# Lower halves of a mixer's weights: a subtraction on VectorE against a scaled copy on ScalarE and an adding DMA

## The chip, the cores and the metric

The program runs on one core of a Trainium2 chip. The metric is the device time of one execution in microseconds, the median of a few runs. TensorE (PE in the rows) multiplies matrices, its weight loads (PEld) run beside the multiplications, VectorE is DVE, ScalarE is ACT, GpSimd is POOL, SyncE is SP.

## The reference

A trunk of two layers over one sequence of 512 tokens with 1024 channels, all in float32. Each layer is

```python
x = x + 0.5 * swiglu_ffn(rmsnorm(x, ffn1_norm[l]), ffn1_w_up[l], ffn1_w_down[l])
x = x + mixer(rmsnorm(x, mix_norm[l]), ...)
x = x + 0.5 * swiglu_ffn(rmsnorm(x, ffn2_norm[l]), ffn2_w_up[l], ffn2_w_down[l])
x = rmsnorm(x, final_norm[l])
```

The mixer multiplies its input with one wide matrix `w_in`, whose columns are q, k and v (three dilation groups of eight heads, 64 wide), the two halves of a gated linear unit (GLU), and two gates, A for the attention branch and one for the convolution branch. Attention is a dilated sliding window. The convolution branch is GLU, a depthwise convolution over 31 tokens, a LayerNorm, a swish and a projection. At the end:

```python
g_attn, g_conv = jnp.split(jax.nn.sigmoid(gates), 2, axis=-1)
return (g_attn * y_attn + g_conv * y_conv) @ w_out
```

## The kernel before, in words

**Three products for one.** TensorE multiplies in a rounded float32 (`F32R`). To keep precision, each operand is split into an upper half, the value rounded, and a lower half, what the rounding left. `mm3` (lines 156 to 159) issues three matmuls for every product: upper times upper, upper weight times lower activation, lower weight times upper activation, all into one accumulator.

**A stage.** Weights come from HBM in pieces of 128 partitions by 1024 numbers (512 KB), that is four row blocks of 256 columns or eight of 128. `stage` (line 140) handles one piece: SyncE's queue issues the load into `raw` (line 151, two buffers), ScalarE copies it rounded into `hi` (line 152, four buffers), VectorE subtracts, `lo = raw - hi` (line 153, four buffers). A stage feeds 24 matmuls of 512 columns. All of it stands under `tc.high_priority(offset=150)`.

**Who calls it.** `proj_cols` (line 218) walks over the row blocks and calls `stage` and `mm3`; the feed-forward layers, the GLU's input, the gates and the three output projections use it or the same loop. `tokens_chunk`, for q, k and v, calls `stage` directly, with two sources side by side for q and k.

**The order of the mixer in the program.** (1) The GLU's input, four column pairs, gate half first (`ps_gg`, `ps_ga`, lines 279 to 292): 16 stages. (2) For each dilation group q, k, v and attention: small matmuls, a masked minimum on VectorE (line 437), the exponential on ScalarE (line 443), transposes, and stores and loads through HBM on GpSimd's queue (`vd`, `V`, `od`, `sd`). (3) The convolution's gate (`ps_gc`), then gate A (`ps_gA`), 8 stages each, with a sigmoid (lines 490 and 503). (4) The depthwise convolution on VectorE, 31 steps for each of 8 blocks (line 516), and the LayerNorm. (5) The attention's parts come back from HBM (`oin`, line 572) and are joined. (6) The convolution's projection (`ps_cp`, 8 stages), attention's (`ps_ap`, 4) and the output's (`ps_o`, 8).

**The order on the chip.** The order within each engine's queue is not the program's: a planner simulates a timeline with a cost for each instruction and writes each engine's queue by priority (place in the program, less the offset above) and by when inputs are ready in that simulation. On the chip each queue then runs strictly in that order. So the convolution's steps stand scattered through VectorE's queue from the GLU on, and the gates' matmuls lie among attention's. Buffers are let go when their last reader is done.

Of the kernel before, what the change touches and what calls it, by code (L numbers as in the profile page):

```python
# [11 lines left out]
F32 = mybir.dt.float32  # L12
F32R = mybir.dt.float32r
AF = mybir.ActivationFunctionType
ALU = mybir.AluOpType
# [4 lines left out]
P = 128  # L20
D = 1024
S = 512
KD = D // P
# [6 lines left out]
AW = NG * NH * HD  # L30
# [14 lines left out]
def trunk(ctx: ExitStack, tc: tile.TileContext, A: dict, out: bass.AP):  # L45
    nc = tc.nc
# [7 lines left out]
    def ps_mm(name):  # L54
        return psp.tile([P, S], F32, tag="mm", name=name, bufs=3)

    def ps_st(name):
        return psp.tile([P, S], F32, tag="st", name=name, bufs=1)

    def ps_at(name):  # L60
        return psp.tile([P, S], F32, tag="at", name=name, bufs=4)
# [63 lines left out]
    def pc(nm, l, k):  # L125
        i = VECS.index(nm) * 16 + l * 8 + k
        return pcol[:, i:i + 1]
# [8 lines left out]
    def uniq(s):  # L136
        cnt[0] += 1
        return f"{s}_{cnt[0]}"

    def stage(*srcs):  # L140

        a, n1 = srcs[0].shape[1], srcs[0].shape[2]
        n = n1 * len(srcs)
        raw = wp.tile([P, 1024], F32, tag="raw", name=uniq("raw"), bufs=2)
        hi = wp.tile([P, 1024], F32R, tag="hi", name=uniq("hi"))
        lo = wp.tile([P, 1024], F32R, tag="lo", name=uniq("lo"))
        m = a * n
        with tc.high_priority(offset=150):
            rv = raw[:, :m].rearrange("p (a n) -> p a n", a=a)
            for i, src in enumerate(srcs):  # L150
                nc.sync.dma_start(rv[:, :, i * n1:(i + 1) * n1], src)
            nc.scalar.activation(hi[:, :m], raw[:, :m], AF.Copy)  # L152
            nc.vector.tensor_sub(lo[:, :m], raw[:, :m], hi[:, :m].bitcast(F32))  # L153
        return (hi[:, :m].rearrange("p (a n) -> p a n", a=a), lo[:, :m].rearrange("p (a n) -> p a n", a=a))

    def mm3(ps, ah, al, bh, bl, first, last):
        nc.tensor.matmul(ps, ah, bh, start=first, stop=False)  # L157
        nc.tensor.matmul(ps, ah, bl, start=False, stop=False)  # L158
        nc.tensor.matmul(ps, al, bh, start=False, stop=last)  # L159
# [5 lines left out]
    def split_to(hi, lo, src):  # L165
        nc.scalar.activation(hi, src, AF.Copy)
        nc.vector.tensor_sub(lo, src, hi.bitcast(F32))
        return hi, lo
# [46 lines left out]
        nc.scalar.activation(R, ps, AF.Copy)  # L215
        return R

    def proj_cols(src, c0, rhs, nk, ps):

        nj = len(ps)  # L220
        step = 8 // nj
        for kk in range(0, nk, step):
            n_ = min(step, nk - kk)
            wh, wl = stage(src[:, kk:kk + n_, c0:c0 + nj * P])
            for j in range(nj):
                for k in range(n_):
                    kg = kk + k
                    mm3(ps[j], wh[:, k, j * P:(j + 1) * P], wl[:, k, j * P:(j + 1) * P], *rhs[kg], kg == 0, kg == nk - 1)
# [35 lines left out]
    def mixer(l, xg, R, rr, after):  # L264
        win = A["w_in"][l].rearrange("(k p) n -> p k n", p=P)
        bin_ = A["b_in"]
        wap = A["w_attn_proj"][l].rearrange("(k p) n -> p k n", p=P)
        wcp = A["w_conv_proj"][l].rearrange("(k p) n -> p k n", p=P)
        wou = A["w_out"][l].rearrange("(k p) n -> p k n", p=P)
        with ExitStack() as mx:  # L270
            mp = mx.enter_context(tc.tile_pool(name=uniq("mix"), bufs=2))

            def slot(tag, bufs, dt=F32, name=None):
                return mp.tile([P, S], dt, tag=tag, name=uniq(name or tag), bufs=bufs)
# [4 lines left out]
            for c in range(4):  # L279
                ga = [ps_mm(uniq("ps_ga")) for _ in range(2)]  # L280
                gg = [ps_at(uniq("ps_gg")) for _ in range(2)]
                proj_cols(win, 3 * AW + D + c * 256, xg, KD, gg)
                proj_cols(win, 3 * AW + c * 256, xg, KD, ga)
                for j in range(2):
                    k = 2 * c + j
                    s = slot("tmp", 7)
                    nc.vector.tensor_mul(s, gg[j], R)
                    nc.scalar.activation(s, s, AF.Sigmoid, bias=bcol[:, l * 32 + 8 + k:l * 32 + 9 + k])
                    ta = slot("tmp", 7)
                    nc.vector.tensor_mul(ta, ga[j], R)  # L290
                    u[k] = slot("big", NB, name="u")
                    nc.vector.scalar_tensor_tensor(u[k], ta, bcol[:, l * 32 + k:l * 32 + k + 1], s, op0=ALU.add, op1=ALU.mult)
# [24 lines left out]
            for i, (nm, f) in enumerate((("q_norm", SCALE), ("k_norm", -1.0))):  # L317
                a = A[nm]
                n = NG * HD
# [163 lines left out]
            for c in range(4):  # L483
                ps = [ps_mm(uniq("ps_gc")) for _ in range(2)]
# [9 lines left out]
            for c in range(4):  # L494
                ps = [ps_mm(uniq("ps_gA")) for _ in range(2)]
                if c % 2 == 0:
                    sg4 = mp.tile([P, 4, S], F32, tag="qk", name=uniq("sga"), bufs=2)
                proj_cols(win, 3 * AW + 2 * D + c * 256, xg, KD, ps)
                for j in range(2):
                    k = 2 * c + j  # L500
                    s = sg4[:, 2 * (c % 2) + j]
                    nc.vector.tensor_mul(s, ps[j], R)
                    nc.scalar.activation(s, s, AF.Sigmoid, bias=bcol[:, l * 32 + 16 + k:l * 32 + 17 + k])
                    sga.append(s)
# [3 lines left out]
            for k in range(KD):  # L508
                a = slot("cv", 2) if k < 2 else slot("big", NB, name="cv")
# [8 lines left out]
            with tc.high_priority(offset=tc.cur_priority - before_units):  # L518
# [4 lines left out]
                ps = ps_st(uniq("ps_mu"))  # L523
# [8 lines left out]
                z = []  # L532
# [10 lines left out]
            m = rp.tile([P, TT, 2, UH], F32, tag="cm", name=uniq("cm"), bufs=1)  # L543
# [15 lines left out]
            ps = ps_st(uniq("ps_cT"))  # L559
# [3 lines left out]
            y = []  # L563
            for pr in range(4):
                acc = None
                for g in range(NG):
                    gp = slice(32 * g, 32 * g + NH)
                    ps = ps_at(uniq("ps_c"))
# [10 lines left out]

            for c in range(4):  # L580
                ps = [(ps_at if c % 2 else ps_mm)(uniq("ps_cp")) for _ in range(2)]
                proj_cols(wcp, c * 256, z, KD, ps)
                for j in range(2):
                    k = 2 * c + j
                    nc.vector.scalar_tensor_tensor(sgc[k], ps[j], pc("b_conv_proj", l, k), sgc[k], op0=ALU.add, op1=ALU.mult)
            mg = []
            for c in range(4):
                ps = [ps_at(uniq("ps_ap")) for _ in range(2)]
                proj_cols(wap, c * 256, y, 4, ps)
                ss = []  # L590
                for j in range(2):
                    k = 2 * c + j
                    s = slot("tmp", 7)
                    nc.vector.tensor_mul(s, ps[j], sga[k])
                    nc.vector.tensor_add(s, s, sgc[k])
                    ss.append(s)
                if c % 2 == 0:
                    ml = mp.tile([P, 4, S], F32R, tag="qk", name=uniq("ml"), bufs=2)
                for j in range(2):
                    mg.append(split_to(slot("sgc", 8, F32R), ml[:, 2 * (c % 2) + j], ss[j]))  # L600
            for ts in ((0, 1), (2, 3), (4, 5), (6,), (7,)):
                ps = [(ps_at if ts[0] in (0, 4, 7) else ps_mm)(uniq("ps_o")) for _ in ts]
                proj_cols(wou, ts[0] * P, mg, KD, ps)
                for k, p in zip(ts, ps):
                    nc.vector.tensor_add(xs[k], xs[k], p)
                    after(k, mp)
# [3 lines left out]
    ps = ps_st(uniq("ps_g"))  # L610
    nc.tensor.transpose(ps[:, :KD], grow, ident[:KD, :KD])
    nc.vector.tensor_copy(gcol, ps[:, :KD])
    xg = []
    for k in range(KD):
        ps = ps_at(uniq("ps_x"))
# [26 lines left out]
    for l in range(DEPTH):  # L642
        nxt, sq = [], [None]
        ffn(l, A["ffn1_w_up"], A["ffn1_w_down"], xg, R, collect("mix_norm", l, nxt, sq), deferred)
        xg, rc, R = nxt, sq[1], sq[2]
        nxt, sq = [], [None]
        mixer(l, xg, R, rc[0], collect("ffn2_norm", l, nxt, sq))
        xg, rc, R = nxt, sq[1], sq[2]

        if l + 1 < DEPTH:  # L650
# [30 lines left out]
            xg, R, deferred = nxt, st["R"], st["x"]  # L681
        else:
# [14 lines left out]
            for tt in range(TT):  # L697
                for kk in range(0, KD, 4):
                    ps = ps_at(uniq("ps_y"))
# [54 lines left out]
```

## Time and profile before

| what | value |
|---|---|
| median of 3 runs | 2669.24 us (2668.72 to 2671.29) |
| the profiled execution's own time | 2669.43 us |
| its span, first to last instruction | 2667.5 us |
| mean granted TensorE clock | 0.992 |
| TensorE busy | 2617.8 us (98%) |
| VectorE busy | 1599.7 us (60%) |
| ScalarE busy | 1005.8 us (38%) |
| GpSimd busy | 110.5 us (4%) |
| DMA moved | 268.65 MB, 101 GB/s over the span |

Busy times are sums over one profiled execution; "us from the start" always means from the first instruction of that execution. Matmuls are pipelined and their ends are modelled, so a busy TensorE need not be at its peak. Layer 0's mixer lies between 377 and about 980 us, layer 1's about 1320 us later.

### The profile page before, as it was taken

Reading aid. Unit: us, or ns where it says so; the run is one execution under the profiler, and the core shown is the slowest. Engines: PE = TensorE matmul, PEld = TensorE weight load, DVE = VectorE, ACT = ScalarE, POOL = GpSimd, SP = SyncE. Lnnn points to the kernel's source line nnn. Section 1 sums busy time; section 2 is a strip of 40 time slices with the busy share of each in tenths; the row PEclk is TensorE's granted clock in tenths of the full one; section 3 lists DMA queues with packets and bytes.
Section 4 is the critical chain, followed back from the end, with each engine's and each line's share of the span. In section 5 each row is a group of like instructions: output and inputs, shape, how many; then the busy total and the mean of one; then the engine's idle time right before and its main releaser. Section 6 shows DMA issues by size and latency. Waiting matters only on the chain.

```text
span 2667.5 us, 30985 instructions
## 1 busy us (share of the span) xinstructions
PE 2617.8 (98%) x12125; PEld 2125.9 (80%) x12125; DVE 1599.7 (60%) x2606; ACT 1005.8 (38%) x1572; POOL 110.5 (4%) x208
## 2 busy tenths in 40 slices
PE   8999999998999999999999999999989999999998
PEld 6888888776877788888888888887767778888887
DVE  4444349999985754443454433599999756444432
ACT  5332232233578242232332322322344963322222
POOL 1000000011011000000000000000011110000000
PEclk9999999999999999999999999999989999999999
DMA  4332333233333333332333322323323343333322
GB/s 155 98 95 91 103 99 105 79 113 97 100 112 110 117 95 96 102 95 95 95 95 95 100 94 93 108 91 114 96 85 121 100 126 103 95 95 96 102 91 75
DMA packets 253778, 268.65 MB, mean 101 GB/s; under 512 B 11624, under 2 KB 238320, under 8 KB 253632
## 3 DMA queue, kind: packets, MB, share of 16 engines
q1 hardware_dynamic: 242112, 234.91, 28.3%
q0 software_dynamic: 11504, 31.76, 4.0%
q8 instruction: 95, 1.56, 0.2%
q14 instruction: 51, 0.42, 0.1%
q10 hardware_dynamic: 16, 0.00, 0.0%
HBM read 251.75 MB, written 14.88 MB: 100 GB/s over the span
## 4 chain that ended last, share of the span: by engine, by line
PE 88%; DVE 7%; ACT 3%; issue 1%; DMA 0%; SPq 0%; ACTq 0%
PE ps_a L158 6%; PE ps_a L159 6%; PE ps_b L157 6%; PE ps_d L157 6%; PE ps_b L158 6%; PE ps_b L159 6%; PE ps_d L159 6%; PE ps_d L158 6%; PE ps_a L157 6%; PE ps_n L158 4%; PE ps_n L157 4%; PE ps_n L159 3%; DVE cv L516 2%; PE ps_cp L158 1%; PE ps_cp L159 1%; PE ps_cp L157 1%
## 5 line engine op out<-in xcount | busy, mean ns | idle before, releaser
L153 DVE TENSOR_TENSOR lo<-raw,hi 128x1024 fp32r<-128x1024 f32 (+1 forms) x448 | 539.2, 1204 | 725.0 <-ACT hi L152 724.0
L152 ACT ACTIVATE hi<-raw 128x1024 fp32r<-128x1024 f32 (+1 forms) x448 | 468.1, 1045 | 1058.3 <-issue 360.2
L516 DVE SCALAR_TENSOR_TENSOR cv<-u,cwc,cv 128x500 f32<-128x500 f32 (+14 forms) x480 | 335.7, 737 | 0.1
L158 PE MATMUL ps_b<-xgl,hi 128*128 128x512 f32 x704 | 275.1, 391 | 0.0
L157 PE MATMUL ps_a<-xgh,hi 128*128 128x512 f32 x704 | 273.5, 389 | 1.1 <-ACT xgh L174 1.1
L159 PE MATMUL ps_a<-xgh,lo 128*128 128x512 f32 x704 | 274.5, 390 | 0.0
L158 PE MATMUL ps_a<-xgl,hi 128*128 128x512 f32 x704 | 274.3, 390 | 0.1
L157 PE MATMUL ps_b<-xgh,hi 128*128 128x512 f32 x704 | 274.0, 389 | 0.0
L159 PE MATMUL ps_b<-xgh,lo 128*128 128x512 f32 x704 | 273.9, 389 | 0.0
L159 PE MATMUL ps_d<-sh,lo 128*128 128x512 f32 x704 | 273.9, 389 | 0.0
L157 PE MATMUL ps_d<-sh,hi 128*128 128x512 f32 x704 | 273.9, 389 | 0.0
L158 PE MATMUL ps_d<-sl,hi 128*128 128x512 f32 x704 | 273.9, 389 | 0.0
L158 PE MATMUL ps_n<-lo,xgh 128*128 128x512 f32 x576 | 228.7, 397 | 3.9 <-DVE lo L153 3.8
L159 PE MATMUL ps_n<-hi,xgl 128*128 128x512 f32 x576 | 225.7, 392 | 0.0
L157 PE MATMUL ps_n<-hi,xgh 128*128 128x512 f32 x576 | 215.8, 395 | 4.7 <-DVE tmp L379 3.4
L157 PEld LDWEIGHTS ps_a<-xgh,hi 128*128 128x128 f32 x704 | 132.0, 188 | 29.0 <-ACT xgh L174 1.5
L158 PEld LDWEIGHTS ps_b<-xgl,hi 128*128 128x128 f32 x704 | 132.2, 188 | 28.0 <-issue 0.7
L159 PEld LDWEIGHTS ps_b<-xgh,lo 128*128 128x128 f32 x704 | 132.2, 188 | 28.0 <-issue 0.7
L158 PEld LDWEIGHTS ps_a<-xgl,hi 128*128 128x128 f32 x704 | 132.2, 188 | 27.9 <-DVE xgl L175 0.5
L159 PEld LDWEIGHTS ps_d<-sh,lo 128*128 128x128 f32 x704 | 132.2, 188 | 27.5
L159 PEld LDWEIGHTS ps_a<-xgh,lo 128*128 128x128 f32 x704 | 132.2, 188 | 27.5 <-issue 0.2
L157 PEld LDWEIGHTS ps_b<-xgh,hi 128*128 128x128 f32 x704 | 132.2, 188 | 27.4
(234 smaller groups left out, 3988.1 us busy)
## 6 DMA issues: line engine op xcount, KB each, us to landing
raw<-in_ffn_w_up_dram SPq DMA_DIRECT2D x176, 512.0 KB, 3.5
raw<-in_w_in_dram SPq DMA_DIRECT2D x88, 512.0 KB, 3.6
raw<-in_ffn_w_down_dram SPq DMA_DIRECT2D x76, 512.0 KB, 3.5
raw<-in_w_in_dram SPq DMA_DIRECT2D x96, 256.0 KB, 3.1
raw<-in_w_conv_proj_dram SPq DMA_DIRECT2D x16, 512.0 KB, 3.5
raw<-in_w_out_dram SPq DMA_DIRECT2D x16, 512.0 KB, 3.5
vd<-tmp POOLq DMA_DIRECT2D x24, 256.0 KB, 2.3
od<-ot POOLq DMA_DIRECT2D x24, 256.0 KB, 3.0
```

Source lines behind the costliest of these rows:

```text
L152: nc.scalar.activation(hi[:, :m], raw[:, :m], AF.Copy)
L153: nc.vector.tensor_sub(lo[:, :m], raw[:, :m], hi[:, :m].bitcast(F32))
L157: nc.tensor.matmul(ps, ah, bh, start=first, stop=False)
L158: nc.tensor.matmul(ps, ah, bl, start=False, stop=False)
L159: nc.tensor.matmul(ps, al, bh, start=False, stop=last)
L516: nc.vector.scalar_tensor_tensor(a[:, t0:t1], u[k][:, t0 + d:t1 + d], cw(l, j, k), a[:, t0:t1], op0=ALU.mult, op1=ALU.add)
```

## The change

`stage` gets a keyword `rest`. With `rest="dma"` the subtraction on VectorE is left out. In its place ScalarE copies the upper half with scale -1 into `lo`, and a DMA from GpSimd's queue reads the same weights from HBM a second time and adds them onto `lo`. `proj_cols` hands the keyword on. Six calls in the mixer pass it: the GLU's two halves, gate A, the convolution's projection, attention's projection and the output's. Left as they were: the feed-forward layers, q, k and v, and the convolution's gate. With 44 stages a layer, 88 of 448 stages change.

```diff
-    def stage(*srcs):
+    def stage(*srcs, rest=None):
...
             nc.scalar.activation(hi[:, :m], raw[:, :m], AF.Copy)
-            nc.vector.tensor_sub(lo[:, :m], raw[:, :m], hi[:, :m].bitcast(F32))
+            if rest == "dma":
+
+                nc.scalar.activation(lo[:, :m], hi[:, :m].bitcast(F32), AF.Copy, scale=-1.0)
+                lv = lo[:, :m].rearrange("p (a n) -> p a n", a=a)
+                for i, src in enumerate(srcs):
+                    nc.gpsimd.dma_start(lv[:, :, i * n1:(i + 1) * n1], src, accum_op=ALU.add)
+            else:
+                nc.vector.tensor_sub(lo[:, :m], raw[:, :m], hi[:, :m].bitcast(F32))
...
-    def proj_cols(src, c0, rhs, nk, ps):
+    def proj_cols(src, c0, rhs, nk, ps, rest=None):
...
-            wh, wl = stage(src[:, kk:kk + n_, c0:c0 + nj * P])
+            wh, wl = stage(src[:, kk:kk + n_, c0:c0 + nj * P], rest=rest)
...
-                proj_cols(win, 3 * AW + D + c * 256, xg, KD, gg)
-                proj_cols(win, 3 * AW + c * 256, xg, KD, ga)
+                proj_cols(win, 3 * AW + D + c * 256, xg, KD, gg, "dma")
+                proj_cols(win, 3 * AW + c * 256, xg, KD, ga, "dma")
...
-                proj_cols(win, 3 * AW + 2 * D + c * 256, xg, KD, ps)
+                proj_cols(win, 3 * AW + 2 * D + c * 256, xg, KD, ps, "dma")
...
-                proj_cols(wcp, c * 256, z, KD, ps)
+                proj_cols(wcp, c * 256, z, KD, ps, "dma")
...
-                proj_cols(wap, c * 256, y, 4, ps)
+                proj_cols(wap, c * 256, y, 4, ps, "dma")
...
-                proj_cols(wou, ts[0] * P, mg, KD, ps)
+                proj_cols(wou, ts[0] * P, mg, KD, ps, "dma")
```

## Rows read from the trace of the kernel before

**Rows 1.** The page, busy time: us, share of the span, instructions of each engine.

```profile
PE 2617.8 (98%) x12125; PEld 2125.9 (80%) x12125; DVE 1599.7 (60%) x2606; ACT 1005.8 (38%) x1572; POOL 110.5 (4%) x208
```

**Rows 2.** Busy time by stretches of layer 0's mixer; columns as in the first line.

```profile
core 0: us, PE busy (x) PEld busy (x) DVE busy (x) ACT busy (x) POOL busy (x), PEclk, DMA share, GB/s
377.00:480.00 103.00, 103.00 (x458) 85.04 (x458) 89.66 (x137) 30.41 (x34) 3.18 (x6) 1.00 0.34 99
394.00:765.00 371.00, 356.66 (x1775) 283.87 (x1774) 360.82 (x690) 144.73 (x290) 35.67 (x66) 0.98 0.35 105
480.00:640.00 160.00, 154.52 (x747) 122.23 (x746) 157.92 (x301) 54.62 (x107) 14.25 (x26) 1.00 0.38 112
640.00:680.00 40.00, 31.58 (x184) 23.13 (x184) 38.31 (x83) 21.68 (x47) 4.00 (x7) 0.79 0.13 35
...
765.00:841.00 76.00, 73.58 (x400) 56.91 (x399) 43.97 (x118) 73.28 (x140) 6.53 (x12) 1.00 0.25 78
850.00:910.00 60.00, 60.00 (x258) 45.35 (x257) 39.53 (x54) 20.36 (x27) 5.38 (x10) 1.00 0.42 137
```

**Rows 3.** Timelines of VectorE and TensorE: start us, us, instruction, idle before and releaser.

```profile
647.92 5.32 DVE L516 SCALAR_TENSOR_TENSOR cv<-u,cwc,cv 128x506 f32<-128x506 f32 x8
...
654.28 0.93 PE L446 MATMUL ps_T<-ident,sp 128*128 128x128 f32 x4 [2.22 <-ACT sp L443]
```

**Rows 4.** Timeline of ScalarE, upper halves of stages of the changed kinds.

```profile
362.57 1.06 ACT L152 ACTIVATE hi<-raw 128x1024 fp32r<-128x1024 f32 x1 [3.23 <-PE ps_d L158]
...
389.37 1.06 ACT L152 ACTIVATE hi<-raw 128x1024 fp32r<-128x1024 f32 x1 [2.22 <-PE ps_gg L158]
...
412.01 1.07 ACT L152 ACTIVATE hi<-raw 128x1024 fp32r<-128x1024 f32 x1 [4.38 <-PE ps_gg L158]
...
417.45 1.06 ACT L152 ACTIVATE hi<-raw 128x1024 fp32r<-128x1024 f32 x1 [3.17 <-PE ps_ga L158]
...
776.79 1.04 ACT L152 ACTIVATE hi<-raw 128x1024 fp32r<-128x1024 f32 x1
```

**Rows 5.** Groups of instructions: count, busy us, mean ns, idle before them and releaser.

```profile
L153 DVE TENSOR_TENSOR lo<-raw,hi 128x1024 fp32r<-128x1024 f32 (+1 forms) x448 | 539.2, 1204 | 725.0 <-ACT hi L152 724.0
L152 ACT ACTIVATE hi<-raw 128x1024 fp32r<-128x1024 f32 (+1 forms) x448 | 468.1, 1045 | 1058.3 <-issue 360.2
```

**Rows 6.** Timeline of VectorE, a lower half and what follows it.

```profile
410.41 1.22 DVE L153 TENSOR_TENSOR lo<-raw,hi 128x1024 fp32r<-128x1024 f32 x1
411.54 1.38 DVE L516 SCALAR_TENSOR_TENSOR cv<-u,cwc,cv 128x499 f32<-128x499 f32 x2
```

**Rows 7.** The chain that ended last, lower halves in ScalarE's full stretches: start, us.

```profile
789.34 1.13 DVE lo L153
...
831.03 1.23 DVE lo L153
...
2115.28 1.23 DVE lo L153
```

**Rows 8.** Groups of instructions on ScalarE from 765 to 850 us.

```profile
L152 ACT ACTIVATE hi<-raw 128x1024 fp32r<-128x1024 f32 x12 | 12.5, 1046 | 0.0
...
L443 ACT ACT_TABLE_LOAD x8 | 10.3, 1283 | 0.1
```

**Rows 9.** Timeline of GpSimd's queue: transfers issued, idle before and releaser.

```profile
802.99 2.17 POOL L471 DMA_DIRECT2D sd<-st  x4 [39.51 <-ACT sp L443]
...
841.52 0.79 POOL L540 DMA_DIRECT2D sa<-sd  x1 [1.70 <-DMA sd<-st]
...
870.50 0.54 POOL L572 DMA_DIRECT2D oin<-od  x1 [17.37 <-DVE oin L577]
```

**Rows 10.** DMA issues: queue, count, KB each, median us from issue to landing.

```profile
raw<-in_w_out_dram SPq DMA_DIRECT2D x16, 512.0 KB, 3.5
...
V<-vd POOLq DMA_DIRECT2D x14, 256.0 KB, 3.4
```

**Rows 11.** Busy time in the fourth microsecond, when the first loads fill the DMA.

```profile
3.00:4.00 1.00, 0.27 (x1) 0.18 (x1) 0.00 (x0) 0.00 (x0) 1.00 (x3) 1.00 1.09 384
```

## The prediction

> **What bounds the kernel now.** I read the page first. TensorE is busy for 98% of the span, VectorE for 60%, ScalarE for 38%, GpSimd for 4% [rows 1]: outside its holes the kernel runs at TensorE's pace, and only a change in a hole can shorten it. The busy time by stretches comes next, since that average hides the stages. Layer 0's mixer runs from 377 us (first matmul of the GLU input) to about 980. In the GLU stretch and again from 850 us TensorE has no hole [rows 2]. It has them between: 5.5 us idle from 480 to 640 and 8.4 from 640 to 680, and in the latter a mean granted clock of 0.79, so for part of it the clock stood at 1.2 instead of 2.4 GHz; 0.21 of 40 us is another 8.4 us. Some 22 us a layer can be had there. From 394 to 765 VectorE is busy 360.82 of 371 us: it is the full engine. From 765 to 841 it is ScalarE, 73.28 of 76 us, with VectorE at 44. Layer 1 repeats the pattern.
>
> The timelines show how a full VectorE makes a hole: a run of eight convolution steps (5.3 us) stands in its queue among the attention's work, and TensorE, a step further on, waits 2.2 us for the exponentials [rows 3]. The convolution is filler, but in an in-order queue it delays what stands behind it.
>
> **The pace of a stage.** In the GLU stretch ScalarE makes an upper half each time TensorE lets go of a buffer, at 412.01 and at 417.45, so 5.44 us a stage [rows 4]. There are four `hi` and four `lo` buffers. The half made at 412.0 is for the stage that starts three stages later, at about 412.0 + 3 × 5.44 = 428.3.
>
> **What is removed.** 88 of 448 subtractions of 1.2 us [rows 5]: 88 × 1.20 = 106 us of VectorE. Only those in a full stretch count. A layer has 44: 16 for the GLU, 8 for gate A, 8 for the convolution's projection, 4 for attention's, 8 for the output. The GLU's first six follow upper halves made from 362.57 to 389.37 us [rows 4], where VectorE still has room; ten fall in the full stretch. Each holds the queue for 1.13 us (the next instruction starts at 411.54 after 410.41 [rows 6]), so 11.3 us. Those from 850 us on buy nothing: TensorE has no hole there. Bounds of what passes on: 0 (only filler moves up) and 11.3. VectorE is busy 97% of the stretch, so I take 0.97 × 11.3 = 11.0 us a layer; the holes of 22 us have room for it.
>
> Gate A's eight follow upper halves made from 776.79 us on [rows 4], in ScalarE's full stretch. The chain that ended last still passes through some: three of 1.13 to 1.23 us in layer 0, two of 1.23 in layer 1 [rows 7]. They stood between a `hi` and the sigmoid's input on VectorE's queue. Removed, that is 3.6 and 2.5, some 3.0 us a layer; lower bound 0, if something equally late takes over.
>
> **What ScalarE gets.** 88 copies with scale −1, same shape as the upper half: 1.045 us [rows 5], 92 us in all. In the GLU stretch ScalarE is busy 30 of 103 us and from 850 to 910 20 of 60 [rows 2]: sixteen and twenty copies there have their cover in its idle time; without it they would cost up to 36 × 1.05 = 38 us a layer. Gate A's eight go into the full stretch: 12 upper halves already cost 12.5 us there and the table loads ahead of the exponentials alone 10.3 [rows 8]. 8 × 1.045 = 8.4 us; what waits behind each copy is the next exponential or sigmoid, and TensorE's transposes and the release of its accumulators behind those. Bounds 0 (the 2.7 us idle there and a slacker TensorE swallow it) and 8.4; with ScalarE 96% busy I take 0.96 × 8.4 = 8.1 us.
>
> **What GpSimd and the DMA get.** 88 transfers of 512 KB, 46 MB more from HBM, each an add onto `lo`, from GpSimd's queue. No row shows an adding DMA, so I bound it.
> - Lateness: from 412.01, upper half (1.07) and copy (1.05) end at about 414.1. The nearest GpSimd issue of as many pieces (four a partition) holds the queue 0.79 us [rows 9]. So 414.9, and need at 428.3: 13.4 us to land. A plain 512 KB load lands in 3.5 us, a 256 KB GpSimd one in 3.4 [rows 10]. Even three times 3.5 is hidden. Cost 0.
> - Rate: the stretch moves 99 GB/s at a DMA share of 0.34 [rows 2], so at 291 GB/s while busy: 512 KB are 1.80 us of the 16 engines. Saturated at the start they moved 384 GB/s [rows 11]: 1.37 us. A stage has 5.44 us for load and add. Floor, add like one copy: 3.6 or 2.7 us together. Ceiling, three passes (weights in, `lo` in, `lo` out), each like a load: 7.2 us at the stretch's rate, 1.76 us too long, or 5.5 at the saturated one. The nearest row is the plain load, so I take the add as hidden: 0.
> - The Trainium skill speaks against the change here: its page "Collectives: The Full Stack", section "The bandwidth ceiling: the fold count and why AG ≠ RS ≠ AR", says that an add in a DMA costs nothing as arithmetic but needs two source reads on one ring, and so gets half the rate of a copy. No row of this case shows it; by it the add would be an estimated 3.6 us, load and add together 5.4 of 5.44 us, and the sum would stay as it is, without room.
> - Queue: an add waits on GpSimd's queue for its copy; behind it stand the tables' gains, the biases, `vd`, `V`, `od`, `sd`, `oin`. In the other direction adds stand behind waits already there: 39.5 us for ScalarE before a statistics store, 17.4 us for VectorE before an `oin` load [rows 9]. The first costs nothing of its own: the copies stand behind the same exponentials on ScalarE. The second comes while four stages are buffered, 13 us; the rest would be 4 us a layer at most. I take 0, as the planner queues by readiness.
>
> `raw` is now let go by the upper half and not 1.2 us later by the subtraction; loads leave earlier and nothing waited for them in these stages: 0.
>
> **The sum.** Per layer −11.0 − 3.0 + 8.1 = −5.9 us, for two layers −11.8. The profiled execution took 2669.43 us (span 2667.5, 1.9 around it), 0.2 above the median: 2669.4 − 11.8 = 2657.6, so 2658.
>
> **Rivals.**
> - *Even.* The relief passes half, 5.5 us, since fewer filler steps don't bring attention's own chain forward, and ScalarE's 8.1 less 3.0 take it back: 2669. For it: the holes at 645 to 667 are a chain of short waits between four engines. Against: VectorE's 97%.
> - *ScalarE decides (slower).* Place: 765 to 841. None of VectorE's relief arrives and no chain step vanishes, so 2 × 8.4 = +17: 2686. It decides as soon as less than 8.4 us a layer is gained elsewhere. For it: ScalarE is at 96% there, with every step behind it. Against: TensorE has 2.4 us idle in the stretch, and five chain steps are on VectorE.
> - *The adds set the pace (slower).* Place: the GLU and everything after gate A, 36 stages a layer back to back. It begins when an add takes over 3.6 to 4.1 us of the engines. At the ceiling 72 × 1.76 = +127, less 11.8: 2784. For it: no room at two reads. Against: the plain row, 1.8.
> - *No change at all* is excluded: 106 us of VectorE do go, and queue orders are planned anew.
>
> **Chances.** Forecast 0.44, even 0.20, ScalarE 0.18, adds 0.18. About 0.2% (5.3 us) is what a measurement can tell from no change. Faster 0.45, same 0.19, slower 0.36: the edge of the even case adds 0.01 to faster, and the rest of it is same. The likeliest case alone runs from 2641 (2 × 14.3 us gained and ScalarE's copies free) to 2664. The range over the cases is 2641 to 2705: it takes in the even case, ScalarE's, and the adds' when they overrun by under half a microsecond a stage; it leaves out a heavy overrun, about 0.15, and a little below.
>
> **What would show it.** 360 subtractions left; 88 copies near 1.05 us; 88 adds of 512 KB landing in 4 to 8 us. Busy: VectorE 106 us less, ScalarE 92 more, GpSimd some 70 more. TensorE still without a hole in the GLU and from 850 on: if matmuls there wait for the DMA, the third rival holds. From the GLU's end to the projection's start about 6 us less a layer, the piece ahead of ScalarE's full stretch shorter by 11 and that stretch longer by 5. If the first piece stays, the step on VectorE's relief was wrong; if the second grows by more than 8, that on ScalarE.

## The result

The changed kernel took 2693.16 us (median of 4 runs, 2690.09 to 2693.55), the kernel before, timed beside it, 2669.57. The ratio is 1.0086, 95% interval [1.0074, 1.0098]: 23.6 us slower, where 2658, faster, was forecast. The time lies inside the range, on the side of the second and third rivals.

The page after: the busy time of the engines, then the DMA queues (packets, MB, share of 16 engines' time). Line numbers from `stage` on are seven higher than before: the copy is L155, the add L158, the subtraction L160.

```profile
PE 2629.1 (98%) x12125; PEld 2132.5 (79%) x12125; DVE 1500.4 (56%) x2518; ACT 1098.8 (41%) x1664; POOL 226.9 (8%) x296
...
q1 hardware_dynamic: 242112, 234.91, 28.2%
q0 software_dynamic: 60016, 77.90, 15.4%
...
L160 DVE TENSOR_TENSOR lo<-raw,hi 128x1024 fp32r<-128x1024 f32 x360 | 431.7, 1200 | 640.6 <-ACT hi L152 639.8
...
L158 POOL DMA_DIRECT2D lo<-in_w_in_dram x48 | 62.3, 1298 | 1297.9 <-ACT lo L155 1251.0
...
lo<-in_w_in_dram POOLq DMA_DIRECT2D x48, 512.0 KB, 7.7
...
raw<-in_w_conv_proj_dram SPq DMA_DIRECT2D x16, 512.0 KB, 6.9
lo<-in_w_conv_proj_dram POOLq DMA_DIRECT2D x16, 512.0 KB, 8.7
```

Against [rows 1], VectorE lost 99 us, ScalarE gained 93, GpSimd 116 (70 were forecast: an issue of an add holds GpSimd 1.3 us, not 0.79). The 88 subtractions are gone, and the program is slower. The same stretches of layer 0's mixer as in [rows 2]:

```profile
core 0: us, PE busy (x) PEld busy (x) DVE busy (x) ACT busy (x) POOL busy (x), PEclk, DMA share, GB/s
377.00:480.00 103.00, 103.00 (x458) 85.01 (x458) 77.21 (x126) 43.57 (x47) 20.40 (x20) 1.00 0.81 168
394.00:765.00 371.00, 356.68 (x1772) 283.08 (x1771) 352.72 (x684) 155.26 (x299) 47.84 (x74) 0.98 0.45 118
480.00:640.00 160.00, 154.72 (x748) 122.14 (x747) 158.61 (x303) 54.79 (x108) 14.38 (x26) 1.00 0.37 112
640.00:680.00 40.00, 31.60 (x185) 23.00 (x183) 38.21 (x83) 21.51 (x47) 4.03 (x7) 0.79 0.12 33
765.00:841.00 76.00, 72.84 (x378) 55.54 (x377) 32.03 (x106) 75.42 (x135) 14.80 (x17) 0.96 0.60 132
850.00:910.00 60.00, 56.95 (x248) 42.91 (x247) 29.74 (x56) 31.42 (x42) 19.23 (x22) 0.97 0.91 208
```

Read it from the top. In the GLU, VectorE is 12 us less busy and TensorE still has no hole: the adds are hidden there, at a DMA share of 0.81. But 480 to 640 and 640 to 680 are as they were, to under a microsecond of every engine: the twelve free microseconds brought nothing forward. The first of attention's bias loads that has to wait for VectorE leaves at 493.50 us before and 494.19 after, attention's last loads of `V` at 760.41 and 761.47. From 765 on the time is lost: ScalarE is now busy 75.42 of 76 us, and from 850 to 910 TensorE has a hole of 3 us that it did not have, with the DMA at 0.91.

**Where the 23.6 us arise.** Three matmuls mark the stretches on TensorE: the first of the convolution's projection (`ps_cp`), of attention's (`ps_ap`) and of the sum that ends the mixer (`ps_ss`). Each is the start of a matmul in the traces, in us:

| | ps_cp | ps_ap | ps_ss | ps_cp, layer 1 | ps_ap | ps_ss |
|---|---|---|---|---|---|---|
| before | 857.38 | 908.85 | 982.07 | 2174.68 | 2227.71 | 2300.93 |
| after | 862.84 | 918.40 | 991.62 | 2191.91 | 2251.64 | 2324.86 |

Up to the projection's start layer 0 loses 5.46 us and layer 1 another 2191.91 − 2174.68 − 9.55 = 7.68: 13.1 in both. Of layer 0's 5.46, some 1.1 are there by the last loads of `V`, the rest arises behind them. Inside the convolution's projection, from `ps_cp` to `ps_ap`, 55.56 for 51.47 and 59.73 for 53.03: 10.8. Behind it nothing. Two places, then: mainly gate A's stretch, and the convolution's projection.

The second hole, in layer 1, seen as TensorE's waits from 2180 to 2255 us (in total, times, longest) and in the chain of work that ended last:

```profile
PE ps_cp L166 <- DMA lo<-in_w_conv_proj_dram: 5.7, 2, 5.4
```

```profile
2201.80 11.28 DMA lo<-in_w_conv_proj_dram
2213.08 0.14 issue
2213.22 0.76 PE ps_cp L166
2213.98 0.43 PE ps_cp L164
...
2219.26 0.23 PE ps_cp L165
```

An add issued at 2201.80 lands 11.28 us later. TensorE idles 5.4 us for it, and then starts a matmul every 0.43 us instead of every 0.23 for 5 us: after the idle time the clock is at 1.2 GHz (granted clock 0.50 from 2213.2 to 2218.2 us). GpSimd's queue in layer 0, to be set beside [rows 9]:

```profile
844.68 2.27 POOL L478 DMA_DIRECT2D sd<-st  x4 [8.34 <-ACT sp L450]
847.68 1.32 POOL L158 DMA_DIRECT2D lo<-in_w_in_dram  x1 [0.73 <-ACT lo L155]
850.04 0.78 POOL L547 DMA_DIRECT2D sa<-sd  x1 [1.05 <-DMA sd<-st]
850.81 1.32 POOL L158 DMA_DIRECT2D lo<-in_w_conv_proj_dram  x1
853.88 1.29 POOL L158 DMA_DIRECT2D lo<-in_w_conv_proj_dram  x1 [1.74 <-ACT ot L468]
854.64 1.68 POOL L470 DMA_DIRECT2D od<-ot  x2
863.79 0.55 POOL L579 DMA_DIRECT2D oin<-od  x1 [7.47 <-DMA od<-ot]
864.59 0.54 POOL L579 DMA_DIRECT2D oin<-od  x1 [0.25 <-DMA od<-ot]
865.13 1.35 POOL L158 DMA_DIRECT2D lo<-in_w_conv_proj_dram  x1
...
870.82 1.27 POOL L158 DMA_DIRECT2D lo<-in_w_conv_proj_dram  x1 [0.97 <-ACT lo L155]
```

The reader is to see that the exponentials end later (they release the last `sd` stores, which go out at 844.68; the load `sa` behind them went at 841.52 before and goes at 850.04 now), and that the projection's third add leaves only at 865.13, when the projection has been running for 2.3 us. It stands behind two `oin` loads that wait 7.47 us for the stores of `od`.

That third add is not the one that TensorE waits for. By the semaphores in the traces TensorE takes the projection's fifth and sixth stages ahead of the third and fourth, whose lower halves it first needs at 895.25 and 900.73 us. The hole in layer 0 is a wait for the fifth add:

```profile
881.24 0.77 PE L166 MATMUL ps_cp<-zh,lo 128*128 128x512 f32 x1 [3.05 <-DMA lo<-in_w_conv_proj_dram]
```

TensorE stands still from 878.19. The fifth add left at 870.82, 7.4 us before, and takes 10.3 us to land. In layer 1 it is the fifth too: the add issued at 2201.80, 6.0 us ahead of TensorE's wait, landing in 11.3. With four `lo` buffers its copy has to wait for the first stage's: in layer 0 the first stage's last matmul starts at 868.17, the copy at 869.46.

### The profile page after: what moved, and what is told of

Read it like the earlier page. It is cut to its first block, busy times and chain, and to the rows that moved or that the text cites. A ratio compares the mean times of both kernels' runs of the same rounds, so it can differ in the third digit from the quotient of the medians.

```text
span 2691.4 us, 31220 instructions
## 1 busy us (share of the span) xinstructions
PE 2629.1 (98%) x12125; PEld 2132.5 (79%) x12125; DVE 1500.4 (56%) x2518; ACT 1098.8 (41%) x1664; POOL 226.9 (8%) x296
## 3 DMA queue, kind: packets, MB, share of 16 engines
q0 software_dynamic: 60016, 77.90, 15.4%
## 4 chain that ended last, share of the span: by engine, by line
PE 84%; DVE 7%; ACT 5%; issue 2%; DMA 2%; POOL 0%; SPq 0%; ACTq 0%; POOLq 0%; DVEq 0%
PE ps_a L166 6%; PE ps_a L165 6%; PE ps_b L164 6%; PE ps_d L166 6%; PE ps_b L166 6%; PE ps_d L165 6%; PE ps_b L165 6%; PE ps_d L164 6%; PE ps_a L164 6%; PE ps_n L165 3%; PE ps_n L164 3%; PE ps_n L166 3%; DVE cv L523 3%; PE ps_gg L166 1%; PE ps_ga L164 1%
## 5 line engine op out<-in xcount | busy, mean ns | idle before, releaser
L160 DVE TENSOR_TENSOR lo<-raw,hi 128x1024 fp32r<-128x1024 f32 x360 | 431.7, 1200 | 640.6 <-ACT hi L152 639.8
L523 DVE SCALAR_TENSOR_TENSOR cv<-u,cwc,cv 128x497 f32<-128x497 f32 (+14 forms) x480 | 333.9, 735 | 0.1
L158 POOL DMA_DIRECT2D lo<-in_w_in_dram x48 | 62.3, 1298 | 1297.9 <-ACT lo L155 1251.0
L165 PEld LDWEIGHTS ps_d<-sl,hi 128*128 128x128 f32 x704 | 132.2, 188 | 27.5
```

Of the source, the lines that this page charges most:

```text
L158: nc.gpsimd.dma_start(lv[:, :, i * n1:(i + 1) * n1], src, accum_op=ALU.add)
L523: nc.vector.scalar_tensor_tensor(a[:, t0:t1], u[k][:, t0 + d:t1 + d], cw(l, j, k), a[:, t0:t1], op0=ALU.mult, op1=ALU.add)
```

## Experiments

Theory after the result: VectorE's relief is worth nothing, ScalarE's copies in gate A's stretch cost, and the adds cost where they come on top of other transfers. Rivals: the adds cost everywhere, gate A's by their lateness rather than ScalarE's copies; or GpSimd's order is to blame.

### The parts one by one

`glu_only` is the change for the GLU alone:

```diff
-                proj_cols(win, 3 * AW + 2 * D + c * 256, xg, KD, ps, "dma")
+                proj_cols(win, 3 * AW + 2 * D + c * 256, xg, KD, ps)
-                proj_cols(wcp, c * 256, z, KD, ps, "dma")
+                proj_cols(wcp, c * 256, z, KD, ps)
-                proj_cols(wap, c * 256, y, 4, ps, "dma")
+                proj_cols(wap, c * 256, y, 4, ps)
-                proj_cols(wou, ts[0] * P, mg, KD, ps, "dma")
+                proj_cols(wou, ts[0] * P, mg, KD, ps)
```

> Only the GLU's 16 stages a layer are made by copy and add. First theory (the profile after): VectorE's relief in the GLU turns into idle time, because the convolution has two accumulators of its own and the next steps can only start when the last GLU block is made; adds are hidden there. So the time stays at that of before, 2669 within 4 us. Rival (the step of the prediction): the relief passes on and only the other stages hide it; then 2669 - 22 = 2647.

Measured 2669.67 us, ratio 1.0 [0.9991, 1.0009]: as the theory had it. So neither a gain from VectorE's relief nor a cost of the GLU's copies and adds. VectorE's timeline at the end of the GLU shows why the relief is lost:

```profile
454.45 1.22 DVE L160 TENSOR_TENSOR lo<-raw,hi 128x1024 fp32r<-128x1024 f32 x1
455.59 0.73 DVE L523 SCALAR_TENSOR_TENSOR cv<-u,cwc,cv 128x497 f32<-128x497 f32 x1
...
458.66 1.23 DVE L160 TENSOR_TENSOR lo<-raw,hi 128x1024 fp32r<-128x1024 f32 x1 [1.74 <-ACT hi L152]
463.16 1.23 DVE L160 TENSOR_TENSOR lo<-raw,hi 128x1024 fp32r<-128x1024 f32 x1 [3.27 <-ACT hi L152]
...
468.53 0.75 DVE L299 SCALAR_TENSOR_TENSOR u<-tmp,bcol,tmp 128x512 f32<-128x512 f32 x1
469.20 1.00 DVE L517 TENSOR_SCALAR cv<-u,cwc,pcol 128x512 f32<-128x512 f32 x2
```

The first two convolution blocks are done at 456 us. The next two (L517) start at 469.20, right behind the last `u`; in between VectorE has no filler left and idles. In the kernel before the first two blocks ended at 470 us, and the next two started behind the last `u` there too (470.70). `cv` has two buffers of its own, and later blocks take one of the eight `big` buffers that hold `u`. The buffer of the first `u` is free from 456 us on, so it is their place in the planned queue that holds the next blocks back; why the planner puts them there no run shows.

`gate_only` changes gate A alone, `gate_copy` does gate A's copy alone, without the add, after which the subtraction overwrites `lo` as before:

```diff
# gate_only
-                proj_cols(win, 3 * AW + D + c * 256, xg, KD, gg, "dma")
-                proj_cols(win, 3 * AW + c * 256, xg, KD, ga, "dma")
+                proj_cols(win, 3 * AW + D + c * 256, xg, KD, gg)
+                proj_cols(win, 3 * AW + c * 256, xg, KD, ga)
...
# gate_copy, as gate_only and
-                for i, src in enumerate(srcs):
-                    nc.gpsimd.dma_start(lv[:, :, i * n1:(i + 1) * n1], src, accum_op=ALU.add)
+                nc.vector.tensor_sub(lo[:, :m], raw[:, :m], hi[:, :m].bitcast(F32))
```

> Only gate A's 8 stages a layer are made by copy and add. First theory: ScalarE is full there, its 8 copies cost some 7 us a layer, so about 2683. Rival (the adds' place in GpSimd's queue and in the DMA does the harm, mostly after gate A): under 2674.

Measured 2684.84 us, ratio 1.0058 [1.0046, 1.0071], near the 2683 of the theory.

> Gate A's 8 stages get ScalarE's scaled copy into lo, but no add: VectorE then overwrites lo by the subtraction of before, so the copy is pure cost. If ScalarE's copies are the cost of gate A, the time is that of the run with gate A alone, within 4 us, some 7 us a layer above before: about 2683. If it is the adds, the time stays near 2669.

Measured 2678.59 us, ratio 1.0032 [1.002, 1.0045]: between the two cases, neither gate A's whole cost nor none. So sixteen copies of 1.05 us cost 8.6 us, 4.3 a layer. Not ScalarE's time alone is in this: the subtraction here waits for the copy, as both write `lo` (VectorE waits 27.9 us for ScalarE's halves from 765 to 850 us, 23.7 in the kernel before), and the queues are planned anew. A copy into a buffer that nobody waits for was not tried. All engines in gate A's stretch of `gate_copy`, and then the groups on ScalarE from 765 to 850 us of the whole change:

```profile
765.00:841.00 76.00, 71.70 (x383) 54.33 (x380) 42.28 (x116) 75.39 (x140) 4.36 (x8) 0.98 0.25 77
```

```profile
L152 ACT ACTIVATE hi<-raw 128x1024 fp32r<-128x1024 f32 x11 | 11.5, 1044 | 0.0
L450 ACT ACT_TABLE_LOAD x8 | 10.3, 1283 | 0.1
L155 ACT ACTIVATE lo<-hi 128x1024 fp32r<-128x1024 f32 x9 | 9.4, 1049 | 0.1
```

ScalarE had 73.28 of 76 us from 765 to 841 [rows 2] and now has 75.4 in both kernels: full, and TensorE is 0.7 to 1.9 us emptier.

`proj_only` changes the three projections alone (the GLU's two calls and gate A's without "dma").

```diff
-                proj_cols(win, 3 * AW + D + c * 256, xg, KD, gg, "dma")
-                proj_cols(win, 3 * AW + c * 256, xg, KD, ga, "dma")
+                proj_cols(win, 3 * AW + D + c * 256, xg, KD, gg)
+                proj_cols(win, 3 * AW + c * 256, xg, KD, ga)
-                proj_cols(win, 3 * AW + 2 * D + c * 256, xg, KD, ps, "dma")
+                proj_cols(win, 3 * AW + 2 * D + c * 256, xg, KD, ps)
```

> Only the three output projections' 20 stages a layer are made by copy and add. First theory: the first adds stand in GpSimd's queue behind oin and od transfers and land late (8 to 11 us), TensorE waits 3 to 5 us a layer: 2675 to 2680. Rival (four buffers hide them, lateness comes only with ScalarE's delay ahead): 2669 within 4 us.

Measured 2671.11 us, ratio 1.0004 [0.9996, 1.0013]: the theory missed, its rival was right. The projections' adds, alone, are hidden. The parts sum to −0.3 + 14.8 + 1.1 ≈ 16, not 23.6.

### The parts in pairs

`no_gate` is the change without gate A, `gate_proj` without the GLU, `glu_gate` without the projections; `glu_gatecopy` is `glu_gate` with gate A's copy alone, then the subtraction.

```diff
# no_gate
-                proj_cols(win, 3 * AW + 2 * D + c * 256, xg, KD, ps, "dma")
+                proj_cols(win, 3 * AW + 2 * D + c * 256, xg, KD, ps)
...
# glu_gatecopy, in stage; gate A calls it with "copy", the projections with nothing
-            if rest == "dma":
+            if rest == "copy":
+                nc.scalar.activation(lo[:, :m], hi[:, :m].bitcast(F32), AF.Copy, scale=-1.0)
+                nc.vector.tensor_sub(lo[:, :m], raw[:, :m], hi[:, :m].bitcast(F32))
+            elif rest == "dma":
```

> GLU and the three output projections by copy and add, gate A as before. If the parts add up: 2670 + 0 + 1 = 2671, within 3 us of before. If the whole change's 8 us beyond the sum of its parts (24 against 0 + 15 + 1) come from GLU and projections together, 2679.

Measured 2671.78 us, ratio 1.0011 [1.0002, 1.002]: these two parts add up.

> Gate A and the three output projections by copy and add, the GLU as before. Theory: gate A's delay of ScalarE and its adds push od, sd and oin into the time of the projection's adds, which are then late; the missing 8 us are theirs: 2692 to 2694, as the whole change. Rival (parts add up): 2670 + 15 + 1 = 2686.

Measured 2684.65 us, ratio 1.0062 [1.0049, 1.0075]: what I expected fell, since gate A and the projections hardly cost more than gate A alone.

> Copy and add for the GLU and gate A; the three projections as before. Gate A alone cost 14.8 us, the GLU alone nothing, the GLU with the projections 2.6, gate A with the projections 15.5; the whole change costs 23.6. If the missing 6 to 8 us come from GLU and gate A together: 2691 to 2693. If they need the projections' adds too (three loads on GpSimd's queue and the DMA after gate A): 2684 to 2686.

Measured 2683.71 us, ratio 1.0056 [1.0043, 1.0069]: additive, so the missing 8 us need all three parts.

> Copy and add for the GLU; for gate A only ScalarE's copy, after which the subtraction makes the lower half as before; projections as before. Gate A's copies alone cost 8.6 us, its adds a further 6. If GLU and gate A meet on ScalarE (copies behind an order that the GLU's relief has changed): 2685 or more. If they meet in the adds (GpSimd's queue, landing): 2678 to 2679, as with gate A's copies alone.

Measured 2684.35 us, ratio 1.0057 [1.0044, 1.0071]. Beside the GLU's adds, gate A's copies (with the subtraction's wait for them) cost 15.5 us by themselves, and taking the add in place of the subtraction changes nothing (14.9). Beside a GLU without adds they cost 8.6, and the adds 6 more. The 8.6 us are measured; what the last 6 us are is open, since either the GLU's change or gate A's adds bring them, but not both together.

### A third accumulator for the convolution

If the two accumulators are what cuts VectorE's relief short, a third should let it pass. It takes the place of one of seven temporaries. `before_cv3` is the kernel before with it, `glu_cv3` is `glu_only` with it, `before_t6` the kernel before with six temporaries and two accumulators.

```diff
-                a = slot("cv", 2) if k < 2 else slot("big", NB, name="cv")
+                a = slot("cv", 3) if k < 3 else slot("big", NB, name="cv")
-                    s = slot("tmp", 7)
+                    s = slot("tmp", 6)
...
```

All other tiles of `tmp` get six buffers likewise.

> The kernel before with a third accumulator for the convolution (cv 3 buffers for blocks 0 to 2), paid for with one buffer fewer of tmp (6 for 7). VectorE is full already in the GLU there, so a third accumulator lets no more steps in: 2670 within 4 us, or a few more for the lost tmp buffer.

Measured 2703.4 us, ratio 1.0129 [1.0115, 1.0143]: a miss.

> The GLU alone by copy and add, with the third accumulator. Theory: the idle time of VectorE in the GLU (some 8 us a layer) fills with convolution steps. If the prediction's step holds (a full VectorE holds TensorE up), the time falls below that of the kernel before with three accumulators by 8 to 20 us. If the convolution is only filler, the VectorE idle time moves behind 765 us and the time stays within 4 us of that kernel.

Measured 2693.87 us, ratio 1.0095 [1.0082, 1.0109]. The instructions of the convolution's step from 394 to 480 us, first in `glu_only`, then in `glu_cv3`:

```profile
L523 DVE SCALAR_TENSOR_TENSOR cv<-u,cwc,cv x72: 727/742/753, 407.2 to 479.1; 128x497 f32<-128x497 f32 x6, 128x498 f32<-128x498 f32 x6, 128x499 f32<-128x499 f32 x6, 128x500 f32<-128x500 f32 x6
```

```profile
L523 DVE SCALAR_TENSOR_TENSOR cv<-u,cwc,cv x85: 731/748/770, 406.1 to 479.9; 128x497 f32<-128x497 f32 x7, 128x498 f32<-128x498 f32 x7, 128x499 f32<-128x499 f32 x6, 128x507 f32<-128x507 f32 x6
```

The kernel before makes 69 steps there and `glu_only` 72: three more for ten subtractions less. With a third accumulator before makes 71 and the GLU's change 85, and now the relief shows in the time: 9.5 us between the two, 4.8 a layer, at the low end of the 8 to 20 expected. But the third accumulator itself costs 34, so this is the relief in another, slower kernel.

> The kernel before with six temporaries in place of seven, nothing else. The variant with a third accumulator and six temporaries took 34 us more than before. If the missing temporary costs it: about 2703. If the third accumulator does (more filler ahead of attention): about 2669 to 2672.

Measured 2669.41 us, ratio 1.0003 [0.9995, 1.0012]. So the temporary is free, and it is the third accumulator that costs: in `before_cv3` VectorE is busy 159.81 of the 160 us from 480 to 640 and TensorE only 145.69, against 157.92 and 154.52 in [rows 2]. Steps of a third block stand among attention's work; that this order is the reason was read from the trace and not tried.

### The convolution's projection

`oin_sp` is the whole change with `oin` issued from SyncE's queue:

```diff
-                    nc.gpsimd.dma_start(o, od[g, pr])
+                    nc.sync.dma_start(o, od[g, pr])
```

> The whole change, with the oin loads issued from SP's queue, so that no add stands behind their wait for od. If GpSimd's queue is what makes gate A's and the projection's adds late: 2680 to 2687 against the whole change's 2693. If the adds are late by their own landing, or the loads of weights now stand behind the same wait on SP: 2693 or more.

Measured 2693.42 us, ratio 1.0093 [1.0079, 1.0107]. The adds no longer stand behind `oin`, and TensorE still waits 4.4 and 5.6 us for one, again the fifth: `oin`'s place on GpSimd's queue is not the cause. The wait for `od` has moved rather than gone: SyncE's queue now stands 11.5 us for it in layer 0, with weights' loads behind.

`no_cp` is the whole change without the convolution's projection, `all_gatecopy` the whole change with gate A's copy alone, then the subtraction (`stage` as in `glu_gatecopy`):

```diff
# no_cp
-                proj_cols(wcp, c * 256, z, KD, ps, "dma")
+                proj_cols(wcp, c * 256, z, KD, ps)
...
# all_gatecopy
-                proj_cols(win, 3 * AW + 2 * D + c * 256, xg, KD, ps, "dma")
+                proj_cols(win, 3 * AW + 2 * D + c * 256, xg, KD, ps, "copy")
```

> The whole change without the convolution's projection, whose lower halves are made by the subtraction as before. In the whole change some 10.8 us of the 24 arise between the first matmul of that projection and the first of attention's. If they come from that projection's own adds: 2682 to 2685, as with GLU and gate A alone. If the adds of the later projections, or the planner's order, cause them: 2690 or more.

Measured 2683.74 us, ratio 1.0054 [1.004, 1.0068].

> The whole change, but gate A's lower halves get only ScalarE's copy and are then made by the subtraction; GLU and projections keep their adds. If the conv projection's adds come late because gate A's adds have filled the DMA engines ahead of them: 2684 to 2687, as with the GLU's adds and gate A's copies alone, and these adds land in 6 to 7 us, not 9. If lateness on ScalarE does it: 2692 or more.

Measured 2687.39 us, ratio 1.0069 [1.0056, 1.0081]; its projection's adds land in 6.6 us, not 8.7. The first came out as the theory had it, the second 0.4 us above its range and far from the rival's 2692. The start of the convolution's projection in both layers, in windows (columns as above): the whole change, `all_gatecopy`, and `glu_gate`, whose projections have no adds:

```profile
850.00:880.00 30.00, 28.19 (x135) 21.11 (x133) 15.53 (x35) 21.48 (x31) 12.55 (x14) 1.00 1.08 237
2180.00:2210.00 30.00, 27.56 (x122) 20.53 (x120) 15.52 (x35) 20.35 (x29) 10.85 (x13) 0.98 1.06 231
```

```profile
850.00:880.00 30.00, 29.98 (x134) 22.85 (x132) 15.19 (x27) 20.83 (x28) 10.94 (x13) 1.00 0.98 218
2180.00:2210.00 30.00, 28.60 (x129) 21.54 (x126) 16.77 (x37) 19.50 (x29) 10.46 (x12) 0.96 1.00 233
```

```profile
850.00:880.00 30.00, 30.00 (x145) 23.54 (x143) 20.96 (x41) 16.87 (x27) 4.22 (x7) 1.00 0.51 144
2180.00:2210.00 30.00, 30.00 (x132) 22.46 (x132) 23.60 (x44) 15.70 (x25) 4.08 (x8) 1.00 0.58 173
```

With the projection's adds the DMA engines are full for 30 us. That alone is no loss, as `no_gate` shows (the stretch ahead, and the same two):

```profile
765.00:850.00 85.00, 81.73 (x444) 62.91 (x442) 45.44 (x131) 80.07 (x151) 10.85 (x18) 1.00 0.30 91
...
850.00:880.00 30.00, 30.00 (x134) 22.67 (x132) 16.48 (x26) 16.99 (x23) 10.44 (x12) 1.00 1.05 242
2180.00:2210.00 30.00, 29.73 (x116) 20.57 (x115) 16.74 (x26) 9.34 (x11) 9.64 (x12) 0.94 0.90 218
```

It is as full, but comes from a share of 0.30 where the whole change comes from 0.56; three of its adds are issued before the projection's first matmul (846.27, 854.38 and 857.20 for 860.12), not two, and they land in 6.2 us. A high share ahead doesn't explain the loss by itself either, as `gate_proj` shows: it comes from 0.58 and loses little.

```profile
765.00:850.00 85.00, 80.88 (x422) 61.61 (x421) 34.81 (x110) 81.05 (x147) 19.29 (x22) 0.96 0.58 127
850.00:910.00 60.00, 59.25 (x243) 44.53 (x242) 30.41 (x57) 30.40 (x41) 17.17 (x21) 0.94 0.85 201
```

What sorts the runs is how long the fifth add takes to land, in layers 0 and 1: 10.3 and 11.3 us in the whole change, 10.0 and 10.9 in `oin_sp`, but 8.0 and 6.4 in `gate_proj`, 7.7 and 8.2 in `all_gatecopy`, 7.0 and 7.5 in `no_gate`, 8.4 and 6.4 in `proj_only`. In the whole change the third and fourth adds and the weights' loads are on the engines just ahead of it (865.13 and 868.56 in layer 0; 857.20 and 864.02 in `no_gate`). This was read from the traces; no run moves the fifth add by itself. By the marks of the traces, over both layers:

| | up to `ps_cp` | `ps_cp` to `ps_ap` | by the medians |
|---|---|---|---|
| glu_only | +2.1 | +1.6 | −0.3 |
| gate_only | +17.0 | −1.6 | +14.8 |
| gate_copy | +8.6 | −1.5 | +8.6 |
| proj_only | +1.2 | +0.8 | +1.1 |
| no_gate | +2.0 | −0.4 | +2.6 |
| glu_gate | +16.6 | −1.6 | +14.9 |
| glu_gatecopy | +21.0 | −1.6 | +15.5 |
| no_cp | +13.4 | −0.8 | +14.6 |
| all_gatecopy | +14.6 | +2.6 | +18.3 |
| gate_proj | +16.3 | +2.9 | +15.5 |
| oin_sp | +13.7 | +10.6 | +24.6 |
| the whole change | +13.1 | +10.8 | +23.6 |

`glu_only` shows 3.7 us in its one profiled execution and none in the median, `glu_gatecopy` 19.5 and 15.5, so differences of up to 4 us mean nothing here (−1.6 is a loss of the kernel before in layer 1, whose granted clock is 0.94 from 2180 to 2210 us). The 10.8 us inside the projection go when its adds go, and shrink to 2.6 when gate A's adds ahead of them go. Without the GLU's change they shrink as much (2.9): all three parts are needed, and why the GLU, 380 us earlier, matters stays open.

## Why the prediction was wrong

**The step that failed is "I take 0.97 × 11.3 = 11.0 us a layer", VectorE's relief.** The runs show 0: the GLU alone 2669.67 against 2670.01. The prediction reasoned that VectorE, 97% busy, sets the pace. But part of the 97% is convolution filler, and filler can only move up as far as its queue order and its accumulators let it: by three steps in layer 0, 2.2 us. The lower bound of the same step, 0, was the case, and for a stronger reason than its "only filler moves up": most of the relief became idle time (from 394 to 765 us VectorE idles 19.4 us in `glu_only`, 10.2 before). The test named ahead, that the first piece stays if this step was wrong, decided it: attention's last loads of `V` leave 1.06 us later, not 11 earlier.

**Gate A's subtractions, −3.0 a layer.** The chain steps of [rows 7] do vanish, but no time goes with them: exchanging subtraction for add beside the GLU's change moves 15.5 to 14.9 us, and without it 8.6 to 14.8. The lower bound of 0 was right or the add costs as much as the step gave.

**ScalarE's copies, +8.1 a layer.** The place was right, and the mechanism as far as `gate_copy` shows it; alone they measure 4.3 a layer, between the bounds 0 and 8.4. With the adds or beside the GLU's change gate A costs 7.4 to 7.8 a layer. The test named for this step was that the second piece grows by more than 8; up to the projection it grew by 5.5 and 7.7.

**The adds, 0.** Right for the GLU (no hole, share 0.81), for attention's and the output's projections, and for the projections alone. Wrong by 10.8 us by the marks (9.0 by the medians, against `no_cp`) in the convolution's projection of the whole change. Its lateness was worked out from the GLU's buffering, 13.4 us ahead of need, and "even three times 3.5" us to land was to be hidden. Here TensorE takes the stages in another order, so the fifth add has 7.4 and 6.0 us, and it lands in 10.3 and 11.3. The `oin` wait that was priced at 4 us a layer at most is not what matters: without it on GpSimd's queue the loss stays.

**The sum.** Per layer −11.0 − 3.0 + 8.1 + 0 = −5.9 was forecast. Measured by the marks are 6.6 up to the projection, all of gate A's and the GLU's terms together, and 5.4 inside it: +12.0 (11.8 by the medians). The time lies inside the range since the range was wide enough for the rivals, not since the forecast's mechanism held.

**The add's price.** GpSimd's queue q0 took 4.0% of the engines' time before and 15.4% after: (0.154 × 2691.4 − 0.040 × 2667.5) / 88 = 3.5 us of the 16 engines for 512 KB; by `glu_only` (8.0% of 2671.1 us, 32 adds) 3.3. A load costs 0.282 × 2691.4 / 448 = 1.69. That is the estimate with two reads, 3.6, and far from the third rival's ceiling. The Trainium skill's page "Collectives: The Full Stack", section "The bandwidth ceiling: the fold count and why AG ≠ RS ≠ AR", gives the adding step of a ring collective half the rate of a copying one, as it needs two source reads; for this add, which is no collective, the trace agrees, at 2.0 to 2.1 times.

**The rivals.** The second, ScalarE decides, is the nearest: no relief arrives, no chain step counts, its place is gate A's stretch, and its 2686 is near what the change takes without the convolution's projection (2683.74). That closeness is in part luck: it prices the copies at 8.4 us a layer, and alone they measure 4.3. It is not the whole: 9 us come from adds, a local form of the third.

**Shown and open.** Shown: the relief's worth of 0, and that in the slower kernel with a third accumulator some of it passes; 8.6 us for gate A's copies with the subtraction behind them; that the projection's loss needs its own adds, and most of it gate A's adds and the GLU's change too; that `oin`'s place on GpSimd's queue is not the cause. Read from the traces and not tried: that the fifth add's landing is the wait. Open: how much of the 8.6 us is ScalarE's time, the 6 us that gate A costs beyond them, and the GLU's part in the projection's loss; these may lie in the planner's queue orders, which differ between these kernels. No version tried is faster than the kernel before.

## What to carry to other kernels

A busy share of 97% doesn't make an engine the bound when part of its queue is filler: ask what the filler can do with a freed microsecond (inputs made, accumulators free) before counting it. Work moved to an engine that has room on average lands in its fullest stretch too, and costs there what it cost nowhere else. A transfer's cover is counted stage by stage: hidden behind an estimated 13 us of buffered stages in one place, the same add has 6 to 7 us where the stages are used out of the order in which they are loaded, and is late there once the DMA engines are full.

## What the runs showed of the hardware

An add onto SBUF of 512 KB took 3.3 to 3.5 us of the 16 DMA engines against 1.69 for a load, landed 5.8 to 9.7 us after its issue by the medians of the groups, up to 11.3 for one (a load 3.5 us in the kernel before), and its issue held GpSimd 1.3 us. After a wait of 5.4 us TensorE started matmuls every 0.43 us for 5 us before it was back at 0.23. The convolution's step took 0.74 us at the median in `glu_only` and 0.75 in `glu_cv3`.
